# Second block of a two-block kernel: sums of squares of MLA keys and queries in four column groups of TensorE, factors and running maxima spread from split rows

## The chip, the cores and the metric

The program runs on one core of a Trainium2 chip (trn2). The metric is device time in microseconds of that core. An execution is a little longer than its profiled span, which runs from the first to the last instruction.

## What is computed

A first block of two mixed layers (sparse attention, a linear recurrence, a convolution) is followed by a second block of one layer. The change is in the second block's mixer, which has two halves that share one input projection: multi-head latent attention (MLA, 4 heads, 256 query tokens, 512 keys from 256 context and 256 latent tokens) and an mLSTM run in both directions.

```python
def mla_prep(cols, g_cq, w_uq, g_ckv, w_ukv, g_qn, g_kn, rope):
    c_q, c_kv, k_rope = ...                       # 256, 128 and 64 columns
    q = (rmsnorm(c_q, g_cq) @ w_uq).reshape(b, n, 4, 192)
    kv = (rmsnorm(c_kv, g_ckv) @ w_ukv).reshape(b, n, 4, 128 + 128)
    k = jnp.concatenate([kv[..., :128], broadcast(k_rope, 4 heads)], axis=-1)
    q = rmsnorm(q, g_qn)                          # over the 192 columns of a head
    k = rmsnorm(k, g_kn)
    ...                                           # rotary part, 64 columns

# mLSTM, per head and direction, with running maximum m_t and cumulative gate cum_f
m_t = jnp.maximum(cum_f + m_prev, max over s <= t of (cum_f[t] - cum_f[s] + ig[s]))
wmat = jnp.exp(dmat - m_t) * (q @ k.T)
```

So each key and each query of each head needs the sum of squares of its 192 columns (128 of its own, 64 of the rotary part, which all heads of a key share), then a factor 1/sqrt(mean + eps). The mixer's output goes through an output projection, a norm and a mixture of experts: for each token and each of 8 heads the 16 best experts are chosen, their rows gathered from HBM, and summed.

## The kernel before

Activations lie with features on partitions and tokens along the free axis. `program` builds everything; `second` is the second block's mixer, `peer` the experts. A scheduler sets the order of each engine from the priorities that `at(us)` gives; the tile pools (`mk`, `slot` by name in SBUF, `psum` by name in PSUM) add the waits for free buffers. PSUM has the names `acc` (two buffers), `acx`, `s` (two), `t`, `o` and `c` (one each). Weights are loaded through SyncE's queue into five buffers `w` and, for the large projections, split into two fp32r halves by ScalarE and VectorE (`wsplit`). Matmuls of the large projections run on such fp32r halves (three products); the smaller matmuls run on plain f32 operands.

**Sums of squares of the keys.** For each head h a matmul gives that head's keys [128 features, 512 tokens] in `acc`; ScalarE writes their squares to `sq` (slots `blk` and `cw2` in turn) and the keys times their gain to `kn`. Then for each of four groups of 128 tokens two matmuls sum over partitions into one column of `ssk` (name `t`), with the squares as the stationary operand and a column of ones moving: one for the head's own part, one (64 rows) for the squared rotary part `skr`. 32 calls in all. The queries do the same into `ssq` (name `o`), 16 calls. The profile has all of them on L256, the helper `mm`.

**Factors.** VectorE scales both sums to `v` [128 tokens, 24], takes 1/sqrt by three Newton steps (`rsqrt`) and gets `rk` (16 columns for the keys, 8 for the queries). To have a key's factor on all partitions, VectorE multiplies the identity by a column of `rk` (`dg`), and a matmul of ones by `dg` gives 128 columns of `bc`. That is done four times for each head; then VectorE multiplies `kn` and the rotary keys (`krz`, slot `g5`, zeroed earlier by GpSimd) by `bc`.

**Running maxima.** `Mr[d]` [8 heads and directions, 512 tokens] holds m_t without the cumulative gate. In `cells`, for each of 8 pairs of head and direction, a matmul with a repeated column of the identity as the stationary operand (8 rows) spreads one row of `Mr` over 128 partitions into `mb` (name `s`, in the profile `s<-pTs,cst`), a bf16 matmul adds the mask, and ScalarE reads the result in several exponentials.

The generators `mla` (scores of a head and a token group, softmax, transposes, product with the values) and `cells` are interleaved by `PATTERN`; `project` (the output projection) follows, then `peer`, whose gathers GpSimd issues.

## Time and profile before

| | |
|---|---|
| runs before | 1406.84, 1406.02, 1400.61 us (median 1406.02) |
| profiled execution | 1406.54 us, span 1404.6 us |
| TensorE busy | 1214.2 us (86% of the span) |
| VectorE busy | 995.6 us (71%) |
| ScalarE busy | 528.6 us (38%) |
| GpSimd busy | 291.9 us (21%) |
| DMA | 387.50 MB, mean 276 GB/s; 268.45 MB of it by the gathers |

Busy time is the time in which an engine works on an instruction; the share is over the whole span, so that it mixes stages with different limits. A view by stretch of time, the chain of what released what, and the rows of single instructions are needed beside it. PE is TensorE, DVE VectorE, ACT ScalarE, POOL GpSimd. A matmul call on plain f32 operands leaves two records in the trace, one on fp32r operands a single one, although both show as f32.

### The profile page before, as it was taken

The numbers are of one execution on the slowest core, as the hardware profiler recorded it, in microseconds if no ns is written. First come the engines' busy times: TensorE is split into PE (matmuls) and PEld (weight loads), VectorE is DVE, ScalarE is ACT, GpSimd is POOL, SyncE is SP. The second block draws the span as 40 slices with busy tenths as digits, with TensorE's granted clock in tenths as the row PEclk, the third lists the DMA queues.
The fourth block names the chain that finished last, engine by engine and source line by source line (L and its number), as shares of the span: only waits on it lengthen the run. The fifth ranks groups of instructions, "written<-read, shape, count | busy, mean of one in ns | idle before, by whom it ended". The sixth has DMA issues, their size and how long they took to land.

```text
span 1404.6 us, 17908 instructions
## 1 busy us (share of the span) xinstructions
PE 1214.2 (86%) x6050; PEld 798.9 (57%) x6050; DVE 995.6 (71%) x2454; ACT 528.6 (38%) x1130; POOL 291.9 (21%) x279
## 2 busy tenths in 40 slices
PE   6999899899979999999898978688868786877787
PEld 5987669698848888856795433243323332323333
DVE  6898865599987674455768766777676767667554
ACT  5635544344754544345453222222222222112211
POOL 0000000000000000000022444334444443443442
PEclk9999999899999987999999998999898999899989
DMA  8677446557403532410459999998999999999996
GB/s 323 193 282 263 168 162 218 169 170 245 133 21 108 165 98 75 132 33 1 151 193 423 421 422 421 421 407 349 421 422 412 422 421 413 414 422 421 417 409 273
DMA packets 71339, 387.50 MB, mean 276 GB/s; under 512 B 8401, under 2 KB 9425, under 8 KB 38226
## 3 DMA queue, kind: packets, MB, share of 16 engines
q0 software_dynamic: 36864, 268.45, 46.4%
q1 hardware_dynamic: 34386, 117.93, 24.8%
q8 instruction: 48, 0.79, 0.2%
q14 instruction: 41, 0.34, 0.1%
HBM read 385.30 MB, written 1.05 MB: 275 GB/s over the span
## 4 chain that ended last, share of the span: by engine, by line
PE 49%; DMA 27%; DVE 8%; issue 8%; POOL 5%; ACT 2%; POOLq 0%; DVEq 0%; SPq 0%; ACTq 0%
DMA G<-uv,eix 24%; PE acc L256 22%; PE acx L256 11%; PE s L256 6%; POOL G L1559 5%; DVE G L1562 4%; PE t L256 3%; PE o L256 2%; DMA wm<-wada 2%; PE c L963 2%; PE s L412 1%; DMA w<-wpq 1%; PE t L259 1%; PE c L256 1%; PE o L645 1%
## 5 line engine op out<-in xcount | busy, mean ns | idle before, releaser
L1562 DVE SCALAR_TENSOR_TENSOR G<-G,hn 128x1024 f32<-128x1024 f32 x256 | 313.5, 1225 | 176.9 <-DMA G<-uv,eix 173.5
L1559 POOL DMA_INDIRECT G<-uv,eix x256 | 284.4, 1111 | 443.0 <-PE o L256 134.4
L323 ACT ACTIVATE wh<-w 128x1024 fp32r<-128x1024 f32 (+2 forms) x142 | 148.5, 1048 | 192.2 <-PE acc L256 120.3
L268 DVE TENSOR_TENSOR wl<-w,wh 128x1024 fp32r<-128x1024 f32 (+2 forms) x142 | 171.5, 1210 | 62.6 <-ACT wh L323 61.3
L256 PE MATMUL t<-G,dg 128*128 128x512 f32 x256 | 146.7, 657 | 69.6 <-ACT dg L1575 69.6
L256 PE MATMUL c<-G,dg 128*128 128x512 f32 x256 | 147.2, 659 | 61.7 <-ACT dg L1575 61.7
L256 PE MATMUL acc<-hh,wh 128*128 128x256 f32 x608 | 178.5, 297 | 11.4 <-ACT wh L323 4.3
L256 PE MATMUL acc<-hh,wl 128*128 128x256 f32 x608 | 178.0, 295 | 2.0 <-DVE wl L268 2.0
L256 PE MATMUL acc<-hl,wh 128*128 128x256 f32 x608 | 166.5, 287 | 1.6 <-DVE hl L268 1.6
L1575 ACT ACTIVATE dg<-cst,w 128x128 f32<-128x128 f32 x256 | 89.4, 394 | 144.9 <-PE o L256 61.6
L256 PE MATMUL o<-G,dg 128*128 128x512 f32 x256 | 141.9, 638 | 0.0
L256 PE MATMUL acx<-G,dg 128*128 128x512 f32 x256 | 141.5, 636 | 0.0
L1566 ACT ACTIVATE s<-s 128x4 f32<-128x4 f32 (+1 forms) x66 | 13.5, 205 | 331.8 <-DVE G L1562 331.7
L256 PEld LDWEIGHTS t<-G,dg 128*128 128x128 f32 x256 | 50.2, 207 | 147.8 <-ACT dg L1575 95.3
L256 PEld LDWEIGHTS acc<-hh,wh 128*128 128x128 f32 x608 | 120.0, 198 | 19.5 <-ACT wh L323 5.1
L256 PEld LDWEIGHTS c<-G,dg 128*128 128x128 f32 x256 | 50.3, 207 | 133.7 <-ACT dg L1575 82.6
L256 PEld LDWEIGHTS acc<-hh,wl 128*128 128x128 f32 x608 | 120.4, 198 | 7.1 <-issue 2.8
L256 PEld LDWEIGHTS acc<-hl,wh 128*128 128x128 f32 x608 | 113.9, 193 | 5.3 <-issue 2.4
L262 DVE SCALAR_TENSOR_TENSOR g<-lu,pb,g 128x256 f32<-128x256 f32 x264 | 115.2, 480 | 0.2
L256 PEld LDWEIGHTS o<-G,dg 128*128 128x128 f32 x256 | 53.0, 207 | 69.5 <-issue 69.5
L256 PEld LDWEIGHTS acx<-G,dg 128*128 128x128 f32 x256 | 52.9, 206 | 68.9 <-issue 68.9
L1054 POOL MEMSET lu<- 128x16 f32 x1 | 0.4, 444 | 401.0 <-DVE g L262 401.0
(494 smaller groups left out, 2000.1 us busy)
## 6 DMA issues: line engine op xcount, KB each, us to landing
w<-w SPq DMA_DIRECT2D x64, 512.0 KB, 4.5
wm<-wada SPq DMA_DIRECT2D x40, 512.0 KB, 5.1
wa<-cw SPq DMA_DIRECT2D x16, 512.0 KB, 5.0
w<-woa SPq DMA_DIRECT2D x16, 512.0 KB, 3.5
w<-wpq SPq DMA_DIRECT2D x16, 512.0 KB, 3.5
w<-w2t SPq DMA_DIRECT2D x12, 512.0 KB, 3.5
w<-wob SPq DMA_DIRECT2D x8, 512.0 KB, 6.2
w<-w2v SPq DMA_DIRECT2D x8, 512.0 KB, 3.9
```

Of the source, the lines that this page charges most:

```text
L256: pe.matmul(out, lhsT, rhs, start=start, stop=stop)
L259: pe.transpose(out, in_, ident)
L262: (e or dve).scalar_tensor_tensor(out, a, s, b, op0=op0, op1=op1)
L268: return (e or dve).tensor_tensor(out, a, b, op=op)
L323: act.activation(hi, w, AF.Copy)
L412: pe.matmul(acc[j:j + 32], ones[:, 0:32], sq[:, q] if square else srcs[i + q], start=i + q < 4, stop=i + q >= n - 4, tile_position=(0, j))
L645: pe.matmul(hps[32 * j:32 * j + 32], blk[:, q4 * 4 + j], w[:, j], start=q4 == 0, stop=q4 == 3, tile_position=(0, 32 * j))
L963: pe.matmul(acc[32 * j:32 * j + 32], sc[:, k], w[:, j], start=k == 0, stop=k == 7, tile_position=(0, 32 * j))
L1559: pool.indirect_dma_start(out=G, out_offset=None, in_=A["uv"], in_offset=bass.IndirectOffsetOnAxis(ap=eix[b][:, h, k:k + 1], axis=0))
L1562: dot = dve.scalar_tensor_tensor(G[:, 0:D], G[:, 0:D], 1.0, hn[b], op0=mul, op1=mul, accum_out=s[:, j:j + 1])
L1566: act.activation(s[:, 0:n], s[:, 0:n], AF.Gelu)
L1575: act.activation(dg, ident, AF.Copy, scale=w[:, j:j + 1])
```

## The change

Keys: the squares of all four heads are kept (`sqk`, slot `g5`). One matmul of a 64 x 128 block of ones with the squared rotary part fills all 128 partitions of `sumk` (name `t`, 512 columns); then, for each head, a matmul of 128 x 32 ones with that head's squares adds to 32 partitions, each in its own column group of the array. ScalarE copies the result to `rowk`. Queries go the same way into `sumq` (name `o`), with the columns `sel0` and `sel1` repeated 32 times for the rotary part of two heads in one tile. Six small matmuls with `bd4` (a block of 32 ones in each of 4 columns) turn the rows into one tile `ss` [128 tokens, 24] with 32 times the sums.

Factors: the 16 columns of `rk` are transposed to `rp` [4, 512] by four transposes, split into two fp32r rows `rkh` and `rkl`, and spread for each head by two fp32r matmuls with a repeated column of an fp32r identity `id8` (4 rows).

Running maxima: `Mr` is split once into `Mh` and `Ml`, and each spread is two fp32r matmuls (8 rows) in place of one on f32.

```diff
+        id8 = slot("sc", 8, F32R)[0:8]
+        act.activation(id8, ident[0:8, 0:8], AF.Copy)
+        Mh = [slot(n, T, F32R)[0:8] for n in ("rows", "ang")]
+        Ml = [slot(n, T, F32R)[0:8] for n in ("silc", "hidr")]
+        for d in range(2):
+            act.activation(Mh[d], Mr[d][:, 256:512], AF.Copy)
+            tt(Ml[d], Mr[d][:, 256:512], Mh[d].bitcast(F32), sub)
...
-        ssk = psum("t", [128, 4, 4])
+        sqk = slot("g5", 2048).rearrange("p (h t) -> p h t", h=4)
+        sumk = psum("t", [128, 512])
...
-            sq = slot(("blk", "cw2")[h % 2], 512)
-            act.activation(sq, acc, AF.Square)
+            act.activation(sqk[:, h], acc, AF.Square)
             act.activation(kn[:, h], acc, AF.Copy, scale=P2("gkn"))
-            for q in range(4):
-                qs = slice(q * 128, q * 128 + 128)
-                mm(ssk[:, h, q:q + 1], sq[:, qs], ones[:, 0:1], True, False)
-                mm(ssk[:, h, q:q + 1], skf[0:64, qs], ones[0:64, 0:1], False, True)
+        mm(sumk, ones[0:64], skf[0:64], True, False)
+        for h in range(4):
+            pe.matmul(sumk[32 * h:32 * h + 32], ones[:, 0:32], sqk[:, h], start=False, stop=True, tile_position=(0, 32 * h))
+        rowk = slot("blk", 512)
+        act.activation(rowk, sumk, AF.Copy)
...
-        ssq = psum("o", [128, 2, 4])
+        sumq = psum("o", [128, T])
+        sqs = []
...
-            for q in range(2):
-                for b in range(2):
-                    bs = slice(b * 128, b * 128 + 128)
-                    mm(ssq[:, b, h + q:h + q + 1], sq[:, q, bs], ones[:, 0:1], True, False)
-                    mm(ssq[:, b, h + q:h + q + 1], sqr[:, h // 2, bs], C(f"sel{q}"), False, True)
+            sqs += [sq[:, 0], sq[:, 1]]
+        for h in range(4):
+            pe.matmul(sumq[32 * h:32 * h + 32], C(f"sel{h % 2}").broadcast_to([128, 32]), sqr[:, h // 2], start=True, stop=False,
+                      tile_position=(0, 32 * h))
+        for h in range(4):
+            pe.matmul(sumq[32 * h:32 * h + 32], ones[:, 0:32], sqs[h], start=False, stop=True, tile_position=(0, 32 * h))
+        rowq = slot("cw2", T)
+        act.activation(rowq, sumq, AF.Copy)
...
+        ss = psum("s", [128, 24])
+        for q in range(4):
+            mm(ss[:, q * 4:q * 4 + 4], rowk[:, q * 128:q * 128 + 128], C("bd4"), True, True)
+        for b in range(2):
+            mm(ss[:, 16 + b * 4:20 + b * 4], rowq[:, b * 128:b * 128 + 128], C("bd4"), True, True)
         v = mk(b1, [128, 24], tag="ssv")
-        ts(v[:, 0:16], ssk.rearrange("p h q -> p (h q)"), 1.0 / 192, EPS, mul, add)
-        ts(v[:, 16:24], ssq.rearrange("p b h -> p (b h)"), 1.0 / 192, EPS, mul, add)
+        ts(v, ss, 1.0 / (32 * 192), EPS, mul, add)
...
+        rp = psum("s", [4, 512])
+        for q in range(4):
+            tr(rp[:, q * 128:q * 128 + 128], rk[:, q * 4:q * 4 + 4], ident)
+        rkh, rkl = slot("blk", 512, F32R)[0:4], slot("cw2", 512, F32R)[0:4]
+        act.activation(rkh, rp, AF.Copy)
+        tt(rkl, rp, rkh.bitcast(F32), sub)
         for h in range(4):
             bc = psum("s", [128, 512])
-            for q in range(4):
-                dg = mk(b1, [128, 128], tag="dg", bufs=2)
-                ts(dg, ident, rk[:, h * 4 + q:h * 4 + q + 1], None, mul)
-                mm(bc[:, q * 128:(q + 1) * 128], ones, dg, True, True)
+            one = id8[0:4, h:h + 1].broadcast_to([4, 128])
+            mm(bc, one, rkh, True, False)
+            mm(bc, one, rkl, False, True)
...
-                        ml_ = Mr[d][:, 256:512].rearrange("p (t c) -> p t c", c=128)
-                        mm(mb, ident[0:8, dh:dh + 1].broadcast_to([8, 128]), ml_[:, :, None, :].broadcast_to([8, 2, 2, 128]),
-                           True, False)
+                        for i, m in enumerate((Mh[d], Ml[d])):
+                            m = m.rearrange("p (t c) -> p t c", c=128)[:, :, None, :].broadcast_to([8, 2, 2, 128])
+                            mm(mb, id8[:, dh:dh + 1].broadcast_to([8, 128]), m, i == 0, False)
```

On TensorE, among the key projections (`acc<-pr,w`) and the query projections (`acx<-tmp2b,w`, `acc<-tmp2b,w`), before:

```order
L256 MATMUL acc_6021<-pr_5215,w_5986 128x512
L256 MATMUL t_5994<-cst_62,blk_5997 128x1
L256 MATMUL t_5994<-cst_62,pr_5217 128x1
...
L256 MATMUL acc_6034<-pr_5215,w_5986 128x512
L256 MATMUL t_5994<-cst_62,cw_991_6010 128x1
...
L256 MATMUL acx_6050<-tmp2b_5218,w_5988 128x256
```

And now (L1245 is the 32-partition matmul on the keys' squares, L1272 the one on the rotary part of the queries):

```order
L256 MATMUL acc_6018<-pr_5215,w_5996 128x512
L256 MATMUL t_6005<-pr_5217,cst_62 128x512
L1245 MATMUL t_6005<-g_992_6004,cst_62 32x512 x2
L256 MATMUL acx_6032<-tmp2b_5218,w_5998 128x256
...
L1245 MATMUL t_6005<-g_992_6004,cst_62 32x512
L256 MATMUL acc_6055<-tmp2b_5218,w_5998 128x256
...
L1245 MATMUL t_6005<-g_992_6004,cst_62 32x512
L256 MATMUL acc_6063<-tmp2b_5218,w_5998 128x256
...
L1272 MATMUL o_6054<-cs_6031,cst_62 32x256 x4
```

The sums stood behind each head's projection, and now stand behind all four, the last two single ones among the query projections.

On TensorE, where the key factors are spread and the first scores (`s<-g,wa`, `s<-g,ow`) begin, before (`acc<-gz,cz` are the cells' products of queries and keys):

```order
L256 MATMUL s_6311<-dg_6318,cst_62 128x128
L256 MATMUL s_6311<-dg_6321,cst_62 128x128
L256 MATMUL acx_6397<-gz_837_5213,cz_5212 128x512
L256 MATMUL acc_6400<-gz_837_5213,cz_5212 128x512
L256 MATMUL s_6326<-dg_6327,cst_62 128x128
L256 MATMUL acc_6403<-gz_837_5213,cz_5212 128x512
L256 MATMUL s_6326<-dg_6330,cst_62 128x128
...
L256 MATMUL s_6359<-g_985_5992,wa_6047 128x512
L256 MATMUL s_6359<-g_1052_6294,ow_6048 128x512
L256 MATMUL s_6341<-dg_6345,cst_62 128x128
L256 MATMUL s_6341<-dg_6348,cst_62 128x128
```

And now:

```order
L256 MATMUL s_6287<-blk_6283,sc_5641 128x512
L256 MATMUL s_6287<-cw_1060_6284,sc_5641 128x512
L256 MATMUL s_6292<-blk_6283,sc_5641 128x512
L256 MATMUL s_6292<-cw_1060_6284,sc_5641 128x512
L256 MATMUL acx_6348<-gz_837_5213,cz_5212 128x512
L256 MATMUL acc_6351<-gz_837_5213,cz_5212 128x512
L256 MATMUL acc_6354<-gz_837_5213,cz_5212 128x512
L256 MATMUL s_6297<-blk_6283,sc_5641 128x512
...
L256 MATMUL s_6302<-cw_1060_6284,sc_5641 128x512
L256 MATMUL s_6310<-g_990_6002,wa_6029 128x512
L256 MATMUL s_6310<-g_1057_6276,ow_6030 128x512
```

The spread of the last head's factors stood behind the first score tile, and now stands ahead of it with all other heads.

## Rows read from the trace of the kernel before

**Rows 1.** The page, section 4: shares of the chain that ended last, by engine.
```profile
PE 49%; DMA 27%; DVE 8%; issue 8%; POOL 5%; ACT 2%; POOLq 0%; DVEq 0%; SPq 0%; ACTq 0%
```

**Rows 2.** Busy time by stretch: stretch, length, engines' busy us, PEclk, DMA share, GB/s.
```profile
541.50:566.83 25.33, 25.33 (x97) 22.30 (x98) 5.67 (x14) 8.58 (x17) 0.00 (x0) 0.66 0.10 26
566.83:597.88 31.05, 31.05 (x152) 24.86 (x152) 15.69 (x36) 12.64 (x17) 0.00 (x0) 1.00 0.47 153
597.88:613.22 15.34, 12.78 (x39) 6.53 (x38) 10.03 (x23) 4.87 (x9) 0.00 (x0) 0.89 0.19 65
613.22:658.63 45.41, 44.73 (x190) 27.53 (x188) 26.81 (x91) 26.74 (x75) 0.96 (x1) 0.89 0.00 0
...
723.70:1404.60 680.90, 540.25 (x1343) 245.23 (x1342) 466.36 (x1158) 164.56 (x408) 284.35 (x256) 0.93 0.99 406
```

**Rows 3.** GpSimd in order of time: the first gather, with its idle time before.
```profile
723.70 1.08 POOL L1559 DMA_INDIRECT G<-uv,eix  x1 [66.88 <-PE acc L256]
```

**Rows 4.** Chain of waits, key and query projections: start, us, engine, tile, line, records.
```profile
542.62 2.29 PE t L256 x16
...
545.96 3.30 PE t L256 x16
549.26 2.86 PE acx L256 x6
552.12 7.92 PE t L256 x32
560.04 1.15 PE acx L256 x2
561.19 4.77 PE acc L256 x16
...
569.11 3.47 PE o L256 x32
```

**Rows 5.** Chain of waits, other pieces at full clock, as prices.
```profile
588.62 4.08 PE acx L256 x18
...
615.09 0.44 PE t L259 x4
...
624.51 1.72 PE s L256 x4
...
652.30 1.73 PE acx L256 x8
...
681.58 0.55 PE s L412 x2
...
685.76 0.56 PE s L412 x4
```

**Rows 6.** Busy time by stretches of 4 us, columns as in rows 2.
```profile
540.00:544.00 4.00, 3.80 (x17) 2.18 (x15) 3.11 (x6) 4.00 (x9) 0.00 (x0) 1.00 0.51 152
...
556.00:560.00 4.00, 4.00 (x17) 3.88 (x17) 0.00 (x0) 0.00 (x0) 0.00 (x0) 0.50 0.00 0
...
616.00:620.00 4.00, 4.00 (x14) 2.22 (x13) 2.98 (x8) 3.81 (x11) 0.00 (x0) 0.79 0.00 0
```

**Rows 7.** Chain of waits, first score tile and first attention product.
```profile
604.33 3.42 PE s L256 x4
...
618.51 3.40 PE acx L256 x8
```

**Rows 8.** VectorE in order of time: query factors; one head's multiplies.
```profile
576.53 0.17 DVE L265 TENSOR_SCALAR rq<-rky 128x8 f32<-128x8 f32 x1
...
585.70 0.69 DVE L268 TENSOR_TENSOR g<-g,s 128x512 f32<-128x512 f32 x1 [0.47 <-PE s L256]
586.30 0.67 DVE L268 TENSOR_TENSOR g<-pr,s 64x512 f32<-64x512 f32 x1
```

**Rows 9.** Groups of matmuls, 526 to 700: names, shapes, records, busy us, mean ns, idle.
```profile
L256 PE MATMUL s<-pTs,cst 8*128 8x512 f32 x16 | 9.6, 680 | 0.7 <-ACT wm L1382 0.7
...
L256 PE MATMUL s<-dg,cst 128*128 128x128 f32 x32 | 5.9, 295 | 1.2 <-DVE dg L265 1.2
```

## The prediction

> **What bounds the kernel now.** Start with the page's shares of the chain that ended last: TensorE holds 49% of it and DMA 27% [rows 1]. That is a mean over two very different halves, so the next view is busy time by stretch [rows 2], cut where the second block's work changes kind. Stage A (541.5 to 566.8) holds the key projection and the query projection with their sums of squares, stage B (to 597.9) the value and output-gate projections, stage C (to 613.2) the spread of the key factors and the first attention scores, stage D (to 658.6) attention and mLSTM cells. In A and B TensorE is busy all the time (25.33 of 25.33 and 31.05 of 31.05 us), in C it idles 2.56 us, in D 0.68 us. DMA share there is 0.47 at most. The last stretch runs from the first expert gather, issued at 723.70 [rows 3], to the end: 680.9 us at a DMA share of 0.99 and 406 GB/s [rows 2]. Its bytes don't change. So the end lies 680.9 us behind the first gather, and the first gather lies behind a chain that is nearly all TensorE: what TensorE is spared before 658, and is not lost to a wait, moves the end by as much.
>
> The profiled execution took 1406.54 us (span 1404.6), the median of the three runs shown is 1406.02. The sum is made against 1406.5.
>
> **Unit prices.** All from the chain [rows 5], at the full clock. A call on plain f32 operands leaves two records, one on fp32r operands a single one. f32 with 512 columns: 1.72 us for two calls, 0.86 each. f32 with 256 columns: 1.73 us for eight records, 0.216 a record, 0.43 a call. fp32r with 512 columns: 4.08 us for 18, 0.227 each. Four transposes: 0.44. For a matmul into 32 of the partitions the nearest rows are the same kind of sums at 681 and 685: one 256-column call takes 0.55 by itself, two in different column groups take 0.56 together. So a lone one costs 0.12 more than a full-width one, and a second in another group next to nothing.
>
> **Stage A.** Removed: 32 calls with one output column for the keys, in three pieces of 2.29, 3.30 and 7.92 us: 13.51 us [rows 4]. Added: the shared rotary part, one 512-column f32 call, 0.86; then four 32-partition calls of 512 columns, in the new order a pair and two single ones among the query projection's matmuls: 0.86 + 0.12 each time, 2.9. Sum 3.8 us (bounds: 2.6 if every 32-partition call hides behind another, 4.8 if the pair runs one after the other). Net -9.7. The four query calls on the rotary part now stand here as well, two pairs at 0.56: +1.1.
>
> The clock. In 540 to 544 it is granted in full, in 556 to 560 at 0.50, its lower level of 1.2 GHz, and in that stretch TensorE is busy 4.00 of 4.00 us [rows 6]. What it did between was a run of one-column matmuls without a gap. The query projection's 24 records lie in the same stretch and pay for it: 2.86 + 1.15 + 4.77 = 8.78 us [rows 4] where 24 x 0.216 = 5.2 is the price at full clock: -3.6 if the clock now stays up, 0 if not. I take -3.6, since the one-column run is gone. The Trainium skill, TensorE: Matmul & The Clock Gate, in its part on the HAM clock gate, puts a fall of the clock down to idle time of TensorE. By that rule these matmuls did not cause the fall, nothing is given back, and the sum ends 3.6 us higher; the row with 4.00 busy out of 4.00 speaks against the rule here.
>
> A new wait. The sum for all heads sits behind four projections whose results ScalarE must read twice (square and scaled copy); the projections of heads 2 and 3 wait for their accumulators, and the sum needs the one buffer `t` that VectorE still reads for the query norm. Nothing in the trace prices this; bounds 0 and 2 us, I take +1.0. The four copies and differences of the 8 x 256 running maxima on ScalarE and VectorE stand ahead of stage A, beside the mLSTM projections' matmuls, and are put at 0; without that cover a few tenths each, +1 in all. Stage A: -9.7 + 1.1 - 3.6 + 1.0 = **-11.2**.
>
> **Stage B.** Removed: 16 one-column query calls, 3.47 us [rows 4], and the first six of the spread's 16 dg calls (128 columns of f32, so half of 0.43 each), 1.3; all 16 leave 32 records and 5.9 us busy, partly overlapped [rows 9]. Added: two pairs of 32-partition query sums, 1.1; six small matmuls into four columns, priced like the removed query calls (3.47 / 16 = 0.22), 1.3; four transposes, 0.4. Net **-2.0** (bounds -0.5 to -3). The longer path to the factors (copy, small matmuls, Newton steps, transposes, copy, difference) is hidden: some 30 matmuls of 0.227 and three of 0.86 stand between the small matmuls and the transposes, over 9 us, against 4.1 for the Newton steps with one weight split among them (from 572.58, the end of the query sums in [rows 4], to the scaled factors [rows 8]); then a 512-column f32 call and twelve at 0.227 (3.6 us) before the spread, against some 1.5 for copy and difference. The memset of `krz` is queued on GpSimd behind the sums, with nothing urgent behind it; its readers come tens of us later.
>
> **Stage C.** Before 15.34 us. In the new order: spread of heads 0 and 1, four fp32r calls, 0.9; three cell products of 0.86, 2.6; heads 2 and 3, 0.9; then the first score tile waits for head 2's product and mask multiply on VectorE, whose starts lie 0.60 apart (585.70 and 586.30) [rows 8]; head 3 follows. I put 0.85 us for it. Then three score tiles at 1.72, with 0.3 of waiting for the exponential: 5.5. Sum 10.7, so **-4.6**. It contains the idle time in front of each dg pair and the first score tile, which ran at half clock: 3.42 us [rows 7] against 1.72 [rows 5]. Bounds -2.5 (clock falls again) and -6 (no waits).
>
> **Stage D.** Eight calls that spread the running maxima, f32 with 8 rows: 9.6 us busy in 16 records [rows 9], about 9.1 of them start to start. As two fp32r calls each they'd take 16 x 0.227 = 3.6: -5.4. Not all of it can be had. Between 616 and 620 ScalarE is busy 3.81 of 4 us [rows 6]: it empties these tiles with exponentials and sets the pace, so the first three calls gain nothing; the other five give about 3.6. The attention products at 618.51 (3.40 us) ran at half clock [rows 7], against 1.73 for the same eight records [rows 5], and those near 640 did too. Shorter runs of 8-row work may keep the clock up, ScalarE's pace may not: I count half of the first, -0.9. Stage D **-4.5** (bounds +1 and -10).
>
> **Sum.** -11.2 - 2.0 - 4.6 - 4.5 = -22.3: 1406.5 - 22.3 = **1384.2 us**, forecast 1384, between 1376 and 1391.
>
> **Rivals.**
> 1. *The clock falls anyway.* Then A gives -7.6, C -2.5, D -3.6: total -15.7, 1391 us. For it: 32-partition and 8-row work remains. Against: the same sums at 681 to 690 stand in a stretch of full speed.
> 2. *The clock rule of idle time.* Only A's -3.6 is missing: 1388 us. Against it stands the busy stretch of [rows 6]. The page is the one named above.
> 3. *fp32r does not shorten few-row matmuls.* No row of the trace has fp32r with 4 or 8 rows or a repeated stationary column. If each such call ran like f32, stage D would cost 16 x 1.05 = 16.8 instead of 9.1 (+7.7 instead of -4.5), and the spread 8 x 0.86 instead of 8 x 0.227 (+5.1): total -5, 1401 us, not to be told from no change. Against: the kernel's fp32r rows with 128 rows all leave one record at 0.227.
> 4. *Slower.* The clock falls at the sums of stage A and stays down through stage B, whose matmuls now run at full clock throughout (0.227 a call). B's 29 us would become 58, and -22 turns into +7: 1413 us. It decides from about 22 us of full-speed work done at half speed. For it: stage A's mean clock of 0.66 [rows 2] means some 17 us at the lower level today (25.33 x 0.34 x 2). Against: it was over by stage B, whose clock is 1.00.
>
> **How the numbers follow.** The forecast and what is near it 0.68, more than 30 us gained 0.04, rival 1 0.11, rival 2 0.08, rival 3 0.05, rival 4 0.04. About 0.5% (7 us) is what a measurement of this kernel can tell from no change: faster 0.90 (the first four), same 0.06 (rival 3 and a little of the rest), slower 0.04. The range takes in rivals 1 and 2 and the bounds of A to D, with the 6 us over which the runs of before spread: 1376 to 1395.
>
> **What would show it.** First gather near 701 instead of 723.7, and 681 us from there to the end. Stage A about 14 us long at a granted clock near 1.0; sums of the keys near 4 us; one record of about 0.23 us for each fp32r call on 8 rows; stage C without a VectorE wait over 1 us; ScalarE busy nearly without a gap in the first 8 us of stage D. It is wrong if the clock of stage A is still near 0.66, if the fp32r calls leave two records, or if the stretch behind the first gather grows by more than 3 us.

## The result and the profile after

The changed kernel took 1384.47 us (median of 4 runs, 1380.43 to 1388.78) against 1403.33 for the kernel before (1400.61 to 1406.84): ratio 0.9863, 95% interval 0.9837 to 0.9888. A second set of runs gave 1384.48 against 1405.88, ratio 0.9846 (0.9815 to 0.9876). The profiled executions are 1384.02 and 1406.54 us long, 22.5 us apart; the forecast was 1384 us and -22.3, counted from that execution of the kernel before. The medians lie 18.9 and 21.4 us apart. The first gather, forecast near 701, went out here:

```profile
700.03 1.08 POOL L1583 DMA_INDIRECT G<-uv,eix  x1 [66.90 <-PE acc L256]
```

The page's shares of the chain that ended last, to be set beside [rows 1], have hardly moved (a mean over two unlike halves tells little of a change in one of them):

```profile
PE 48%; DMA 30%; DVE 8%; issue 7%; POOL 4%; ACT 2%; POOLq 0%; DVEq 0%; SPq 0%; ACTq 0%
```

Busy time by stretch, columns as in [rows 2]: stages A, B, C and D, the stretch to the first gather, and the gathers. From here on the cuts are starts of matmul records on TensorE that can be found in every kernel (third key projection, first product of the value and output-gate projections, first record behind the last of those, first transpose of the attention, first product with the weights behind it). For the kernel before this gives 24.99, 31.24, 15.50 and 45.41 us.

```profile
539.13:552.66 13.53, 13.29 (x51) 6.48 (x51) 5.74 (x14) 8.86 (x18) 1.80 (x1) 1.00 0.18 54
552.66:582.52 29.86, 29.86 (x133) 21.64 (x131) 13.55 (x27) 13.65 (x19) 0.00 (x0) 1.00 0.43 149
582.52:594.85 12.33, 10.59 (x28) 4.63 (x28) 9.50 (x17) 4.83 (x9) 0.00 (x0) 1.00 0.26 95
594.85:634.95 40.10, 38.65 (x190) 25.93 (x188) 26.53 (x91) 26.85 (x75) 0.95 (x1) 0.96 0.01 1
634.95:700.03 65.08, 59.75 (x450) 54.58 (x449) 44.66 (x129) 29.88 (x58) 0.00 (x0) 0.95 0.31 106
700.03:1382.20 682.17, 542.52 (x1344) 245.53 (x1342) 465.50 (x1158) 164.62 (x408) 288.68 (x256) 0.92 0.99 406
```

A lost 11.5 us, B 1.4, C 3.2, D 5.3. Two differences are not put down to the change, since they vary as much from one execution to the next (table below): stage A began 2.4 us earlier, and the gathers took 1.3 us longer at the same 406 GB/s.

The chain of waits through stage A, which answers to [rows 4]:

```profile
540.50 1.12 PE acc L256 x2
541.62 1.05 PE t L256 x2
542.68 0.98 PE t L1245 x4
543.66 1.92 PE acx L256 x8
545.58 0.98 PE t L1245 x2
546.56 1.92 PE acc L256 x8
548.48 0.98 PE t L1245 x2
549.46 1.92 PE acc L256 x8
551.38 0.57 PE o L1272 x8
```

The key sums are the four `t` pieces (one of L256, three of L1245): 1.05 + 3 x 0.98 = 3.99 us where 13.51 stood. Two calls in different column groups (0.98 for four records) cost what one costs (0.98 for two). The three pieces of the query projection take 5.76 us; they took 8.78.

TensorE in order of time where the spreads stand: four fp32r calls on 4 rows, the first score tile, and two spreads of running maxima on 8 rows.

```profile
582.52 0.50 PE L256 MATMUL s<-blk,sc 4*128 4x512 f32 x1
582.86 0.39 PE L256 MATMUL s<-cw,sc 4*128 4x512 f32 x1
583.09 0.38 PE L256 MATMUL s<-blk,sc 4*128 4x512 f32 x1
583.31 0.39 PE L256 MATMUL s<-cw,sc 4*128 4x512 f32 x1
...
589.08 1.12 PE L256 MATMUL s<-g,wa 128*128 128x512 f32 x2 [1.50 <-DVE g L268]
...
595.50 0.49 PE L256 MATMUL s<-rows,sc 8*128 8x512 f32 x1
595.83 0.38 PE L256 MATMUL s<-silc,sc 8*128 8x512 f32 x1
596.15 0.28 PE L256 MATMUL s<-mkp,identb 128*128 128x256 bf16 x1
...
597.75 0.49 PE L256 MATMUL s<-rows,sc 8*128 8x512 f32 x1 [0.71 <-ACT blk L1337]
```

An fp32r call on few rows leaves one record, but price is read from start to start: 0.34 for the first behind calls of another size (582.52 to 582.86), 0.23 for the next, and 0.32 for the one before a call of 128 rows (595.83 to 596.15). A pair on 8 rows thus costs 0.65, not 0.454.

### The profile page after: what moved, and what is told of

Read it like the earlier page. It is cut to its first block, busy times and chain, and to the rows that moved or that the text cites. A ratio compares the mean times of both kernels' runs of the same rounds, so it can differ in the third digit from the quotient of the medians.

```text
span 1382.2 us, 17743 instructions
## 1 busy us (share of the span) xinstructions
PE 1193.9 (86%) x5972; PEld 775.5 (56%) x5972; DVE 991.6 (72%) x2440; ACT 530.5 (38%) x1136; POOL 296.2 (21%) x279
## 3 DMA queue, kind: packets, MB, share of 16 engines
q0 software_dynamic: 36864, 268.45, 47.1%
HBM read 385.30 MB, written 1.05 MB: 280 GB/s over the span
## 4 chain that ended last, share of the span: by engine, by line
PE 48%; DMA 30%; DVE 8%; issue 7%; POOL 4%; ACT 2%; POOLq 0%; DVEq 0%; SPq 0%; ACTq 0%
DMA G<-uv,eix 27%; PE acc L256 22%; PE acx L256 11%; PE s L256 5%; POOL G L1583 4%; DVE G L1586 4%; DMA wm<-wada 2%; PE c L963 2%; PE t L256 2%; PE o L256 2%; PE s L412 1%; PE t L259 1%; PE c L256 1%; PE o L811 1%; PE o L645 1%
## 5 line engine op out<-in xcount | busy, mean ns | idle before, releaser
L1583 POOL DMA_INDIRECT G<-uv,eix x256 | 288.7, 1128 | 438.8 <-PE acx L256 140.6
L256 PE MATMUL t<-G,dg 128*128 128x512 f32 x256 | 146.5, 656 | 70.1 <-ACT dg L1599 70.1
L256 PE MATMUL c<-G,dg 128*128 128x512 f32 x256 | 148.1, 663 | 62.4 <-ACT dg L1599 62.4
L256 PE MATMUL acc<-hh,wh 128*128 128x256 f32 x608 | 178.5, 297 | 7.8 <-ACT hh L468 3.6
L256 PE MATMUL acc<-hh,wl 128*128 128x256 f32 x608 | 176.8, 293 | 2.7 <-DVE wl L268 2.0
L256 PE MATMUL acc<-hl,wh 128*128 128x256 f32 x608 | 166.5, 287 | 1.2 <-DVE hl L268 1.1
L256 PE MATMUL acx<-G,dg 128*128 128x512 f32 x256 | 143.1, 643 | 0.0
L256 PE MATMUL o<-G,dg 128*128 128x512 f32 x256 | 141.2, 635 | 0.0
L1590 ACT ACTIVATE s<-s 128x4 f32<-128x4 f32 (+1 forms) x66 | 13.5, 205 | 325.2 <-DVE G L1586 325.2
L256 PEld LDWEIGHTS t<-G,dg 128*128 128x128 f32 x256 | 50.2, 206 | 149.9 <-ACT dg L1599 96.0
L256 PEld LDWEIGHTS acc<-hh,wh 128*128 128x128 f32 x608 | 119.3, 197 | 16.2 <-issue 4.7
L256 PEld LDWEIGHTS c<-G,dg 128*128 128x128 f32 x256 | 50.5, 209 | 135.1 <-ACT dg L1599 83.3
L256 PEld LDWEIGHTS acc<-hh,wl 128*128 128x128 f32 x608 | 119.7, 197 | 7.1 <-DVE wl L268 2.9
L256 PEld LDWEIGHTS acc<-hl,wh 128*128 128x128 f32 x608 | 113.8, 193 | 5.8 <-issue 3.2
L256 PEld LDWEIGHTS o<-G,dg 128*128 128x128 f32 x256 | 53.2, 208 | 69.9 <-issue 69.9
L256 PEld LDWEIGHTS acx<-G,dg 128*128 128x128 f32 x256 | 52.7, 206 | 69.0 <-issue 69.0
```

What stands on the lines that cost most here:

```text
L256: pe.matmul(out, lhsT, rhs, start=start, stop=stop)
L1583: pool.indirect_dma_start(out=G, out_offset=None, in_=A["uv"], in_offset=bass.IndirectOffsetOnAxis(ap=eix[b][:, h, k:k + 1], axis=0))
```

## The experiments

Stage lengths of all profiled executions, us (A to gather: from the start of stage A to the first gather). Each kernel has one profiled execution, the changed one two. Medians are of all runs; each ratio, with its 95% interval, is against the kernel before in the same set of runs, whose medians lie between 1403.3 and 1405.9 us:

| kernel | median us | ratio | A starts | A | B | C | D | to gather | A to gather | gathers |
|---|---|---|---|---|---|---|---|---|---|---|
| before | 1403.3 | | 541.5 | 25.0 | 31.2 | 15.5 | 45.4 | 65.1 | 182.2 | 680.9 |
| changed | 1384.5 | 0.986 (0.984-0.989) | 539.1 | 13.5 | 29.9 | 12.3 | 40.1 | 65.1 | 160.9 | 682.2 |
| changed, again | 1384.5 | 0.985 (0.982-0.988) | 540.7 | 13.5 | 29.8 | 12.3 | 41.6 | 65.1 | 162.4 | 679.3 |
| keys' sums only | 1400.6 | 0.997 (0.994-1.000) | 540.1 | 12.4 | 33.0 | 19.2 | 47.1 | 65.0 | 176.6 | 681.9 |
| both sums only | 1394.7 | 0.991 (0.989-0.994) | 543.3 | 13.1 | 29.7 | 19.0 | 43.8 | 65.0 | 170.6 | 684.7 |
| maxima only | 1400.2 | 0.997 (0.994-0.999) | 539.8 | 23.9 | 31.3 | 14.1 | 41.5 | 65.1 | 175.8 | 679.3 |
| spread only | 1399.8 | 0.997 (0.996-0.999) | 540.8 | 25.0 | 32.2 | 9.4 | 45.4 | 65.0 | 177.0 | 680.7 |
| spread undone | 1393.5 | 0.993 (0.990-0.996) | 539.6 | 13.5 | 29.8 | 18.8 | 40.0 | 65.7 | 167.8 | 681.3 |
| keys undone | 1393.9 | 0.992 (0.990-0.995) | 541.8 | 27.8 | 30.2 | 9.4 | 36.1 | 70.0 | 173.4 | 677.1 |
| no rotary calls | 1392.4 | 0.990 (0.987-0.994) | 541.9 | 11.3 | 34.5 | 15.6 | 47.1 | 64.9 | 173.3 | 680.3 |
| wide sums | 1396.5 | 0.996 (0.993-0.998) | 536.7 | 21.0 | 31.3 | 15.1 | 40.4 | 65.1 | 172.9 | 682.2 |
| sums together | 1383.5 | 0.984 (0.981-0.986) | 544.0 | 11.9 | 29.0 | 12.3 | 40.1 | 65.1 | 158.4 | 684.6 |
| factor buffers | 1386.9 | 0.987 (0.984-0.990) | 536.7 | 13.5 | 29.9 | 14.5 | 35.9 | 70.0 | 163.8 | 680.5 |
| together and stacked | 1379.7 | 0.982 (0.980-0.985) | 540.6 | 11.9 | 29.0 | 13.5 | 34.5 | 70.1 | 159.0 | 679.7 |

In three kernels some 5 us of cell work came to stand behind the cut between D and the next stretch, so their D is short and the next 70; the column "A to gather" is free of that.

**The same kernel again.**

> The changed kernel once more, to see which of the differences between two traces are the kernel's and which come from one execution to the next. Expected if the stages are the kernel's: stage A 13.5 us (first value projection at 13.5 behind the third key projection), B 29.9, C 12.3, D 40.1 within 0.5 us, the clock at half in 616 to 624 and nowhere else between 524 and 660. Expected of the stretch ahead of stage A, where the traced executions so far start stage A between 539.1 and 541.9 us: another time within that range, as nothing of the change stands there but 5 short instructions on ScalarE and VectorE. The gathers' stretch (677 to 682 us in six traces) also differs by up to 3 us.

A, B and C came out alike to 0.02 us, so they are the kernel's. D did not: 41.59 against 40.10, where 40.1 within 0.5 was expected, and the half clock stood elsewhere. The first execution's two rows by stretches of 4 us:

```profile
616.00:620.00 4.00, 3.32 (x15) 2.40 (x14) 3.12 (x19) 3.92 (x11) 0.00 (x0) 0.79 0.00 0
620.00:624.00 4.00, 4.00 (x14) 2.30 (x13) 1.87 (x6) 1.99 (x5) 0.00 (x0) 0.78 0.00 0
```

and the second's, where 616 to 624 is at full clock:

```profile
600.00:604.00 4.00, 4.00 (x13) 2.72 (x13) 2.76 (x8) 3.30 (x10) 0.00 (x0) 0.50 0.01 2
604.00:608.00 4.00, 4.00 (x16) 3.06 (x16) 1.28 (x4) 1.09 (x3) 0.00 (x0) 0.65 0.02 4
```

Over the table, A starts between 536.7 and 544.0 us and the gathers take 677.1 to 684.7. One trace against one trace therefore says nothing on 2 or 3 us outside the stages.

**One part alone.** Keys' sums by column groups in the kernel before (the query's one-column calls stay):

```diff
-                mm(ssk[:, h, q:q + 1], sq[:, qs], ones[:, 0:1], True, False)
-                mm(ssk[:, h, q:q + 1], skf[0:64, qs], ones[0:64, 0:1], False, True)
+        mm(sumk, ones[0:64], skf[0:64], True, False)
+            pe.matmul(sumk[32 * h:32 * h + 32], ones[:, 0:32], sqk[:, h], start=False, stop=True, tile_position=(0, 32 * h))
```

> The kernel before with one part of the change: the keys' sums of squares by ones in four column groups; the queries' sums, the spread of the key factors and of the running maxima stay as they were. Theory (the run of one-column matmuls costs its 13.5 us and drags the clock down with it): the sums cost about 4.0 us, the 24 records of the query projection come down from 8.8 to 5.8 us, stage A goes from 25.3 to 12.5-13.0 us at a granted clock of 1.00; stage B grows by up to 0.9 us for four small matmuls; stages C and D stay within 1 us. Total 11 to 13 us less, near 1391. Rival (the clock falls in this stage for another reason, idle time for one): the projection keeps its 8.8 us, stage A is 16 us, total 8 to 9 us less, near 1395. The changed kernel reached stage A 2.4 us earlier than the kernel before; if that belongs to the copies of the running maxima, it is absent here.

Stage A did what was expected (12.4 us, clock 1.00), but the total fell by 4 us, not 12: B, C and D gave 7 back. The query's 16 one-column calls, at full clock in [rows 4], now brought the clock down. Their piece of the chain:

```profile
555.07 3.76 PE o L256 x32
```

The stretch of 4 us that begins in it, columns as in [rows 2]:

```profile
556.00:560.00 4.00, 4.00 (x26) 3.81 (x26) 0.17 (x1) 0.00 (x0) 0.00 (x0) 0.76 0.01 2
```

Both sums, factors and maxima left as they were:

> The kernel before with both sums (keys and queries) by ones in column groups; the key factors still spread by 16 scaled identities, the running maxima as before. The run with the keys' sums alone gained 12.6 us in stage A and had lost 7 of them by the end of stage D: the clock fell at the query's one-column calls (0.76 and 0.81 of full in 556 to 564, where the kernel before has them at full clock right behind its low stretch) and again in stage C, 0.53 to 0.62 between 592 and 600. Theory (one-column and few-column runs each bring the clock down, and once it has been up for a while it falls at the next one): without the query's one-column calls stage B is near 30-31 us at a clock of 1.00; the 16 scaled identities of stage C still have waits and half clock, stage C 15 to 19 us; D 45 to 47. Total 10 to 14 us less than before, near 1392. Rival (the fall in stage C follows from how long the clock had been up and comes in any kernel): stage C's clock is as low as in the keys-only run, 0.82, and total near 1396. Second rival (the query's calls don't matter): B as in the keys-only run, 33 us.

B is back at 29.7 with a clock of 1.00, as the theory had it (the second rival falls), but C is 19.0 again, at the clock of 0.82 that the first rival named. So a long C does not hang on the query's calls. Nor does it come in any kernel, as that rival has it: C is at 1.00 in the changed kernel and with the spread alone.

Maxima only (`id8`, `Mh`, `Ml` and the two calls of line 1395 added to the kernel before):

> The kernel before with the other end of the change alone: the running maxima split into two fp32r halves and spread by two 8-row calls each; sums and key factors stay as they were. Theory (stage D is TensorE's in part, and the eight f32 calls cost it 9.1 us against about 5.2 for sixteen fp32r calls in pairs of 0.65): stage D 3.5 to 5.5 us shorter, stages A to C as before within 1 us, total 4 to 5 us less, near 1398. Rival 1 (ScalarE, which empties these tiles, sets the pace of the stage): D within 1 us of before, total no different, 1403. Rival 2 (what the changed kernel gained ahead of stage A comes with these copies): another 2.4 us less ahead of stage A, total near 1396. If the clock of the first attention product is tied to stage D's 8-row work alone, the product takes 1.7 us here too, not 3.4.

D is 3.9 us shorter: ScalarE does not set the pace of the whole stage (rival 1 falls). C and A are 1.4 and 1.1 us shorter by clock alone (C at 1.00 in place of 0.89, A at 0.71 for 0.66). The clock has a share in D too. Stage D here, and in the wide sums (below), where the maxima are spread by f32 calls as before:

```profile
609.01:650.51 41.50, 40.16 (x189) 26.95 (x188) 26.54 (x91) 26.65 (x75) 0.95 (x1) 0.92 0.00 1
604.07:644.50 40.43, 39.75 (x190) 24.73 (x188) 26.81 (x91) 26.72 (x75) 0.96 (x1) 1.00 0.00 0
```

With the clock up throughout, the f32 calls leave a D as short as the changed kernel's. TensorE is busy nearly all the time in D, so its length times its mean clock estimates what it would take at full clock. That gives 40.0 to 40.5 us in the six kernels with f32 calls (before, keys' sums only, both sums only, spread only, no rotary calls, wide sums) and 38.2 to 38.5 in the five executions with fp32r calls and the same cut (changed twice, maxima only, spread undone, sums together). So the new calls are worth about 2 us of stage D. The rest, with the same f32 calls 40.4 in one execution and 47.1 in another, is clock. The half clock of the first attention product [rows 7] does not hang on the f32 form of the 8-row calls alone; it is there with the fp32r calls too:

```profile
614.67 3.41 PE acx L256 x8
```

Spread only (transposes, `rkh`, `rkl` and the fp32r calls in place of the 16 `dg` calls):

> The kernel before with the third part alone: the key factors spread by transposes and fp32r calls on 4 rows; sums and running maxima stay. Theory (the 16 scaled identities cost stage C its waits for VectorE, their absence leaves one wait of 1 to 1.5 us): stage C from 15.5 to 12-13 us at a clock near 1.00, B about 1 us shorter, A as before (25.0), D within what the clock does there (45 to 47). Total 4 to 6 us less, near 1400. Rival (without the faster sums the factors come too late and the chain of copy, transposes and copy shows): stage C no shorter than 15 us. The parts by themselves so far, up to the first gather and behind stage A's start: both sums -11.6, maxima -6.4; the whole change -21.3. If the parts add up, this one has to bring about -3.

C fell from 15.5 to 9.4 (12 to 13 was expected), and B rose by 0.9 where it was to fall by 1: the spread of heads 0 and 1 stands in B here. VectorE's multiplies and the weight split of 1.23 us then run beside the last projection matmuls, and the wait that was expected in C is gone, 0.16 us of idle time against 1.74 in the changed kernel, where all four heads stand in C. Stage C by busy time, spread only:

```profile
598.03:607.40 9.37, 9.21 (x23) 4.05 (x23) 7.36 (x15) 5.44 (x10) 0.00 (x0) 1.00 0.31 115
```

and in the changed kernel with the spread undone (below):

```profile
582.93:601.74 18.81, 15.32 (x47) 8.34 (x46) 12.31 (x29) 5.03 (x9) 0.00 (x0) 0.82 0.19 70
```

The parts add up, as far as single executions can show it. Over "A to gather" both sums bring -11.6, the maxima -6.4, the spread -5.2: -23.2, against -21.3 and -19.8 for the whole. By the ratios: -0.9, -0.35 and -0.26 make -1.5%, against -1.4 and -1.5%.

**One part undone.**

> The changed kernel with the spread undone: the key factors again by 16 scaled identities, sums and maxima changed. It shows what the spread is worth beside the other two parts. Theory (the spread frees stage C of five waits for VectorE, and with faster sums they would show most): stage C 18 to 19 us at a clock near 0.8 as in the run with the sums alone, instead of 12.3; B 29.9, A 13.5, D 40 to 42; total 6 to 7 us more than the changed kernel, near 1391. Rival (the long stage C of the sums-only run was the clock's chance): stage C 15 us, total 2 to 3 us more.

Keys', queries' sums and maxima changed, `dg` calls as before: as the theory had it, 18.8 us in stage C and 6.9 more to the gather (5.4 more than in the second execution of the changed kernel). The median is 9 us higher, where 6 to 7 was expected. Without the new spread 28 of its 32 records stand in stage C (20 in the kernel before), with five idle stretches of TensorE for VectorE's scaled identities and multiplies, and the clock falls to 0.50 behind them.

> The changed kernel with one part undone: the keys' sums again by 32 one-column calls; the queries' sums, the factors and the maxima stay changed. Theory: the one-column run and its half clock come back, the calls take about 13 us and the query projection 8 to 9, stage A goes from 13.9 to 24-26 us at a clock near 0.66; total 10 to 12 us more than the changed kernel, near 1395. Rival (the clock has nothing to do with these calls): the calls take 7 to 8 us at full clock, the projection stays at 5.8, stage A is 18 us, total 4 to 5 us more, near 1389. Stages C and D should stay at 12.3 and 40.1 us in either case.

The one-column run brought the half clock back, 27.8 us at 0.63 (24 to 26 was expected); total 9 to 10 us above the changed kernel. That goes through the whole table: in the four kernels with the run of 32 one-column calls (before, maxima only, spread only, this one) stage A has a mean clock of 0.63 to 0.71, in the ten other executions 1.00. C was to stay at 12.3 and is 9.4: as with the spread alone, heads 0 and 1 are spread in B. That suggests that the wait in the changed kernel's C hangs on that place in the order; no run has the earlier place together with the faster sums, so it is not shown.

**What brings the clock down in stage A.** First half of the calls taken out:

> The kernel before without the 16 one-column calls on the rotary part (this leaves the rotary part out of the keys' norms); 16 one-column calls on the latent part remain, in groups of four or eight between projection matmuls. It asks whether one-column calls lower the clock whatever their number, and what one costs where no 64-row call stands between. Theory (a long run of them lowers the clock): with half of them, and other matmuls between, the clock stays up, a call costs 0.22 us, 3.5 us in all, the query projection 5.8: stage A near 11.7 us, total 12 to 14 us less than before, near 1390. Rival 1 (any one-column calls lower it): the 16 calls take 5 to 7 us and the projection stays at 8 to 9, stage A 16 to 19 us, total 7 to 9 less, near 1395. Rival 2 (a call costs 0.29 at full clock, as the first eight do in the kernel before, whatever stands between): 4.6 us for the sixteen.

The chain: eight records, four calls, in 0.79 us, so 0.20 a call where 64-row calls stand between cost 0.29; further on the query's calls.

```profile
543.06 0.79 PE t L256 x8
...
554.91 4.65 PE o L256 x32
```

Stage A stayed at 1.00 and took 11.3 us, as the theory had it, but now the clock fell at the query's calls (4.65 us, 0.62 and 0.53 from 556 to 564), and B paid 3 us. Fewer calls moved the fall; they did not end it. So the number of calls was kept and only their width changed:

```diff
+        pool.memset(Z, 0.0)
+        pool.memset(Z[:, 127:128], 1.0)
-                mm(ssk[:, h, q:q + 1], sq[:, qs], ones[:, 0:1], True, False)
-                mm(ssk[:, h, q:q + 1], skf[0:64, qs], ones[0:64, 0:1], False, True)
+                c = 127 - (h * 4 + q)
+                mm(ssk, sq[:, qs], Z[:, c:c + 128], h + q == 0, False)
+                mm(ssk, skf[0:64, qs], Z[0:64, c:c + 128], False, h + q == 6)
```

> The kernel before, order and number of matmuls untouched, with one size changed: each of the keys' 32 sum calls streams 128 columns in place of one (127 of them zeros, so the sums stay what they were). In the kernel before a 128-column call costs 0.22 us at full clock, as a one-column call does, so the calls' price is the same and TensorE stays as busy; only how much of it is used differs. Theory (one-column calls make the clock fall because they give the array next to nothing to do): the clock stays at 1.00 from 542 to 562, a call of the run costs about 0.3 us, 32 of them 9 to 10, the query projection 5.8, stage A 17.5 to 18.5 instead of 25.0 us; total 6 to 8 us less, near 1398. Rival 1 (the clock falls for what the calls are otherwise, their number, the change between 128 and 64 rows, or what went before): clock 0.66 and stage A 25 us as before. Rival 2 (idle time of TensorE decides): likewise no difference.

The chain of waits:

```profile
537.81 3.14 PE t L256 x16
...
546.63 6.47 PE t L256 x32
...
560.36 3.47 PE o L256 x32
```

Two stretches of 4 us in the middle of the run:

```profile
548.00:552.00 4.00, 4.00 (x21) 2.88 (x20) 0.00 (x0) 0.00 (x0) 0.00 (x0) 1.00 0.00 0
552.00:556.00 4.00, 4.00 (x20) 3.30 (x20) 0.60 (x2) 1.68 (x4) 1.81 (x1) 1.00 0.00 0
```

In the kernel before, the stretch in which the clock falls and the next:

```profile
544.00:548.00 4.00, 4.00 (x20) 3.41 (x20) 2.82 (x7) 2.56 (x6) 0.00 (x0) 0.83 0.22 90
548.00:552.00 4.00, 4.00 (x14) 3.42 (x13) 0.07 (x1) 1.18 (x2) 0.00 (x0) 0.50 0.00 0
```

The same order and number of matmuls (the sums also become one accumulation over a whole tile, and GpSimd fills the operand first), TensorE busy without a gap in both kernels, and the clock is 1.00 where the kernel before has 0.50. So it was not the number of the calls or their change between 128 and 64 rows (rival 1), and not idle time (rival 2), but their one-column form. Two things stay open. One execution was profiled, and what went before, also part of rival 1, differed in it: the clock had not dipped ahead of stage A, while it was at 0.50 for some us between 513 and 525 in the thirteen other executions. With that dip behind them, the four executions with the one-column run fall again in stage A and the nine without it do not, which speaks against that part. And a wider call also lasts longer, so that weight loads (PEld) fill less of the time, 2.88 and 3.30 us of 4 against 3.42 and, in [rows 6], 3.88; the runs do not part the two.

The price was off: 0.40 us a call (6.47 / 16), not 0.3, so stage A is 21.0 us and not 17.5 to 18.5. The median fell by 8 us, as forecast, but in the profiled execution 5.0 of the 9.3 us up to the gather are stage D's, which ran at full clock though the edit does not touch it; the total says little on the sums.

The Trainium skill, TensorE: Matmul & The Clock Gate, in its part on the HAM clock gate, names idle time as what lowers the clock; here it was lowered with TensorE busy 4.00 of 4.00 us. Elsewhere a trace fits the rule: in stage C of the keys' sums only, TensorE is busy 2.24 of 4 us in 588 to 592 and the clock is 0.53 in 592 to 596. But in the second execution of the changed kernel it is busy 2.51 of 4 us in 588 to 592, and the clock stays at 1.00 up to 599.

What stays open: the query's 16 one-column calls fell to half clock in two kernels (keys' sums only, no rotary calls) and ran in full (3.47) in the four others that have them (before, maxima only, spread only, wide sums). In the first three of these the clock had come back from its low stretch about 5 us earlier; in the wide sums it had not fallen at all. No run tells why.

**Can stage C's wait be had?** Heads 2 and 3 of the spread into buffers of their own:

```diff
-            bc = psum("s", [128, 512])
+            bc = psum(("s", "s", "c", "t")[h], [128, 512])
```

> The changed kernel with one edit: the spread factors of heads 2 and 3 go into two other PSUM buffers instead of taking back the two that heads 0 and 1 and then the first score tiles use. Theory (the 1.50 us that TensorE idles ahead of the first score tile is a wait for that buffer, which VectorE frees only after a weight split of 1.23 us and two output gates that stand ahead of head 2's multiply): the wait goes, the eight few-row calls stand in one row at 0.23 each behind the first, stage C from 12.3 to 10.5-11 us. Rival (the score tiles wait for VectorE's own pace, whatever buffer is used): the wait moves to another tile and stage C stays above 12 us.

The rival is right: the first score tiles start at once, but the third waits, for ScalarE's exponential, which waits for the same VectorE work, and a half-clock stretch follows; stage C is 14.5 us, and 163.8 us to the gather are no gain. TensorE in order of time, the third tile:

```profile
590.75 1.12 PE L256 MATMUL s<-g,wa 128*128 128x512 f32 x2 [2.37 <-ACT blk L1337]
```

**A better version.** Key sums held back behind the last query projection:

```diff
+        with tc.issue_after(lastq.ins):
+            for h in range(4):
+                pe.matmul(sumk[32 * h:32 * h + 32], ones[:, 0:32], sqk[:, h], start=False, stop=True, tile_position=(0, 32 * h))
```

> The changed kernel with the four 32-partition key sums held back until the last query projection, so that all four column groups stand in one row on TensorE instead of a pair and two single ones. Theory (calls in different column groups run together, each group's row costs what one call costs: 0.98 us at 512 columns): one piece of 0.98 to 1.2 us instead of three of 0.98, and the rest of stage A unchanged, 13.5 to about 11.7 us (first projection to the first value projection); nothing later is late, since the factors are wanted 28 us on. Total 1.5 to 2 us less than the changed kernel. Rival (only two groups run together): the row takes 1.96 us, stage A 12.5. The difference in total is smaller than the runs spread, so the stage decides.

All four groups run as one, and A and B are 2.5 us shorter together (40.9 for 43.4; B's 0.9 of it was not expected); in the total that is below what the runs tell apart. The piece of the chain:

```profile
552.89 0.99 PE t L1269 x8
```

Then the two halves in one operand, rows 0 and 32, one call instead of two:

```diff
-            mm(bc, one, rkh, True, False)
-            mm(bc, one, rkl, False, True)
+            mm(bc, id40[0:36, h:h + 1].broadcast_to([36, 128]), rks, True, True)
```

> A version that should be a little faster than the changed kernel: the four key sums in one row (as in the run with the sums together, which measured 2.5 us less over stages A and B), and the two fp32r halves of a spread value put into rows 0 and 32 of one operand, so that one call does what two did. Theory: stages A and B 41 us together instead of 43.4; each of the 8 maxima calls in stage D 0.33 us shorter where TensorE sets the pace, each of the 4 factor calls 0.23; ScalarE gets three more short copies ahead of stage A and one in B, hidden. Total 3 to 5 us less than the changed kernel, near 1380. Rival (in stage D ScalarE sets the pace, and the zeros cost as much as is saved): A and B as in the sums-together run, D 40 us, near 1382, which the runs hardly tell from 1384.

1379.7 us (1376.1 to 1381.1), the lowest median of all, ratio 0.9821 against 0.9846 and 0.9863; the intervals overlap. Its trace doesn't show a gain from the stacking: 159.0 us to the gather, 158.4 without it. A stacked call costs 0.42 us (595.60 to 596.02) where the pair cost 0.65, but the wait for VectorE ahead of the first score tile grew, and that tile ran at half clock (TensorE in order of time).

```profile
587.84 1.67 PE L256 MATMUL s<-g,wa 128*128 128x512 f32 x2 [2.17 <-DVE g L268]
...
595.60 0.49 PE L256 MATMUL s<-rows,sc 40*128 40x512 f32 x1
596.02 0.28 PE L256 MATMUL s<-mkp,identb 128*128 128x256 bf16 x1
```

## Why the prediction was right, step by step

- **The forecast.** 1384 us, measured 1384.47. The prediction names two upper ends of its range, 1391 with the sum and 1395 with the chances; the time lies in both.
- **What bounds the kernel.** Right: what TensorE was spared up to 635 us arrived at the first gather whole (65.07 and 65.08 us between), and the gathers kept their length within the scatter.
- **Stage A, -11.2, measured -11.5.** Sums of the keys 3.99 us for 3.8. The query calls on the rotary part 0.57 for 1.1: they stood four in a row and ran as one. The projection 5.76 for 5.2; each of its three pieces now stands between calls of another size, which would explain 0.2 us a piece. The clock -3.0 for -3.6. The new wait 0.24 for 1.0. The cause given for the clock, that the one-column run brings it down, is shown by the undone keys and the wide sums; rival 2 (the rule of idle time) would have left the 3 us and falls. The clock's share is larger than the prediction says: it counts all 13.51 us as the calls' own price, while 32 calls at the 0.31 us of those ahead of the fall would be 10 us, so that some 3.5 us of it (an estimate) is clock too.
- **Stage B, -2.0, measured -1.4.** No wait appeared, the longer path to the factors was hidden. Most of the 0.6 us stands behind the two pairs of query sums, where two fp32r calls took 0.66 and three 0.89 instead of 0.45 and 0.68:

```profile
554.74 0.66 PE acx L256 x2
...
559.15 0.89 PE acc L256 x3
```

- **Stage C, -4.6, measured -3.2.** The mechanism was right, the wait for VectorE mis-sized: 1.50 us for 0.85, because a weight split of 1.23 us stood ahead of head 2's multiply. "No VectorE wait over 1 us" was one of the prediction's signs, and it failed. The eight calls took 2.3 us for 1.8, the cell products 2.8 for 2.6, the three score tiles 5.8 for 5.5. What the prediction did not see: with faster sums and the old spread this stage would have grown to 19 us, so the spread is worth 6.4 us over B and C beside the sums and 5.2 without them.
- **Stage D, -4.5, measured -5.3 and -3.8.** The number came out, the two terms did not. The calls were put at -3.6 and are worth about 2 us at full clock (see the maxima alone): a pair costs 0.65 us, not 0.454, which is 1.6 us over the eight. The clock was put at -0.9 and by the same estimate brought the rest, 3.4 us in the first execution and 1.7 in the second. The reason given for it, shorter runs of 8-row work, is not borne out: with the maxima alone the first attention product stayed at half clock, and with the f32 calls of before stage D of the wide sums ran at 1.00 throughout. What moves the half clock in D stays open.
- **Rivals.** Rival 1, the falling clock, did not come in the changed kernel: A, B and C are at 1.00 and D at 0.96 and 0.92. It is real in the parts taken alone: the keys' sums alone lost 7 of their 12.6 us to it and to the waits. Rival 3 falls (one record a call), rival 4 too (B at 1.00).
- **Luck.** In D a calls' term too large and a clock term too small offset each other, and the clock there differs from one execution to the next. The start of A (-2.4) and the gathers (+1.3) come from run to run and nearly cancelled. The sum was made against one execution of 1406.5 us, 3 above the median of its set: the median moved by 19 to 21 us, the forecast said 22.

## What to carry to other kernels

Sums over partitions that landed in one column kept TensorE busy and brought its clock down here; asked for as rows, with ones on 32 columns of the array in different column groups, they cost a quarter with the clock back in full (13.5 + 3.0 us to 4.0), and with all groups in one row half of that again. Before a part of a change is dropped as small, try it beside the others: what it frees may only be wanted once the stage ahead has become faster. Price few-row calls from start to start with the neighbours that they will have, and take stages rather than totals where parts of a few us are compared. Before a stage's gain is put down to an edit, set its length beside its granted clock: in stage D the clock moved more than the edit did.

## What the runs showed of the hardware that was not expected

- A run of 32 one-column f32 calls brought the granted clock to 0.50 with TensorE busy 4.00 of 4.00 us; the same run at 128 columns a call kept 1.00 and took 0.40 us a call where alternating 128 and 64 rows, against 0.29 to 0.31 for one column at full clock and 0.52 at half.
- A change of call size costs about 0.1 us on each side (0.34 and 0.32 against 0.23). One-column f32 calls show it too: 0.20 us each in a row, 0.29 to 0.31 where 128 and 64 rows alternate. The Trainium skill, TensorEngine Tiling (Array Packing), Key Properties, says that changing the tiling mode drains TensorE; the extra 0.1 us at a change in rows fits that, and no trace shows the drain itself.
- The same program's half-clock stretch stood at 616 to 624 in one execution and at 600 to 608 in another, and cost stage D 1.5 us more in the second. With the same f32 calls stage D took 40.4 to 47.1 us, at a mean clock of 1.00 to 0.85.
